# An encoder layer whose two feed-forward parts become 2x2x2 block products with seven multiplications, the residual stream with tokens on partitions

## The chip, the cores and the metric

The kernel runs on one core of a Trainium2 chip. Five engines work from their own instruction streams: PE multiplies matrices, DVE and ACT do elementwise work (only they and PE reach PSUM), POOL does elementwise work on SBUF alone, SP issues the transfers. The metric is the device time of one execution in microseconds (us).

## The reference, cut to what matters

512 tokens (two groups of 256) of 1024 channels go through one layer. The change concerns the two feed-forward parts and what touches the residual `x`; attention, the state-space branch and the memory branch stay.

```python
D_MODEL, D_FF = 1024, 2816
def rms_norm(x, g):
    y = xf * lax.rsqrt(jnp.mean(xf * xf, axis=-1, keepdims=True) + RMS_EPS)
    return y * g
def swiglu(x, w_gate, w_up, w_down):
    return (jax.nn.silu(x @ w_gate) * (x @ w_up)) @ w_down

x = x + 0.5 * swiglu(rms_norm(x, ffn1_norm), ffn1_w_gate, ffn1_w_up, ffn1_w_down)
u = rms_norm(x, mix_norm); proj = u @ w_in
...
x = x + merged @ w_out
x = x + 0.5 * swiglu(rms_norm(x, ffn2_norm), ffn2_w_gate, ffn2_w_up, ffn2_w_down)
```

## The kernel before

**Precision.** Every large product is made of three matmuls: each float32 operand is split into `hi`, its value rounded to the type fp32r, and `lo`, the rest; the product is hi·hi + hi·lo + lo·hi. A weight chunk of 128 x 1024 is loaded (`wr`, L211), cast to `wh` on ACT (L224) and the rest `wl = wr - wh` is made on DVE (L225, recorded under the helper's line L160). `ahead` (L215) does this up to two chunks ahead of PE. `wh` and `wl` have three buffers each, so the split of chunk c+2 can begin only when PE has finished chunk c-1.

**Layout.** Channels are on partitions and all 512 tokens are columns. `unit` (L372) computes 128 output channels by 512 tokens: the weights are the stationary operand, the activations stream 512 columns. `quad` (L388) is the other way round, tokens stationary and 512 weight columns streaming, one bank for each of four blocks of 128 tokens.

**Feed-forward.** Each of the two has two halves of 11 blocks of 128 hidden channels. For each block `do_g` (L406) and `do_u` (L421) take 8 k-tiles of 3 matmuls; then eight `do_d` units (L439) take 11 k-tiles of 3. The norm is not applied first: the gain alone scales x (`split_gain`, L186), matmuls begin at once, and the row factor R (`t_R`, L362: sums of squares over partitions by matmuls, a chain of small DVE operations in `rsqrt`, L192, spread back by matmuls) multiplies the results in the evacuations.

**Order.** `run` (L262) goes through a plan: a unit is written, then the evacuation of the unit before it, then one step of each side task (`step`, L233). The engines do not run in this written order: a scheduler of the framework orders each engine's instructions by when their inputs are ready, with the written order as priority. After ffn1 come the memory keys and values (`km`, `vm`), which `t_mem` (L455) prepares beside the last down products, then `dt`, which needs u (`t_u`, L478). Ahead of ffn2 stand the eight units of `do_wo` (L807). PSUM has eight banks, five for `unit` and `quad` results and three for the rest.

Of the kernel before, what the change touches and what calls it, by code (L numbers as in the profile page):

```python
# [14 lines left out]
D = 1024  # L15
NT = 512
KD = 8
DFF = 2816
HALF = 11
# [8 lines left out]

def make_plan():
    """Order in which the weights are used: (kind, key, [(matrix, k0, nk, column, width)])."""  # L30
    s = []

    def a(kind, key, mat, col, ks=((0, 8),), m=128):
        s.append((kind, key, [(mat, k0, nk, col, m) for k0, nk in ks]))

    def quad(kind, q, mat, col):
        for c in range(4):
            s.append((kind, (q, c), [(mat, 2 * c, 2, col, 512)]))

    def ffn(f):  # L40
        for hf in range(2):
            for j in range(HALF * hf, HALF * hf + HALF):
                a("g", (f, j), f + "_w_gate", j * 128)
                a("u", (f, j), f + "_w_up", j * 128)
            k0 = HALF * hf
            for m in range(8):
                a("d", (f, hf, m), f + "_w_down", m * 128, ks=((k0, 6), (k0 + 6, 5)))
# [37 lines left out]
    for m in range(8):  # L85
        a("wo", m, "w_out", m * 128)
# [5 lines left out]
CHUNKS = [c for _, _, cs in PLAN for c in cs]  # L92
OFFS = np.concatenate([[0], np.cumsum([128 * nk * m for _, _, nk, _, m in CHUNKS])])
WTOTAL = int(OFFS[-1])
# [3 lines left out]
for _name, _w in (("ffn1", 8), ("mix", 8), ("mem", 8), ("ffn2", 8), ("cw", 160), ("cb", 32), ("qn", 1), ("kn", 1),  # L98
                  ("mqn", 2), ("mkn", 2), ("sn", 16), ("dd", 16), ("dtb", 1), ("al", 1)):
    PCOLS[_name] = _n  # L100
    _n += _w
# [4 lines left out]
KEEP, EARLY = 6, 4  # L106
TEMPS = set("rw e f e2 ca cb xt yq dg jk jn pm pmT nt npT bi st qbd kT nv mq ut xgh xgl".split())


class Layer:  # L110
    def __init__(self, tc, ctx, aps):
# [5 lines left out]
        self.pg = pool("pg", 58)  # L117
        self.pt = pool("pt", 21)
        self.pw = pool("pw", 3)
# [6 lines left out]
        self.hold = False  # L126
# [4 lines left out]
        self.raw, self.split = {}, {}  # L131
        self.n_dma = self.n_split = 0
# [12 lines left out]
    def bank(self, p="m"):  # L145
        pl = self.pm if p in "mq" else self.pd
# [6 lines left out]
    def link(self, n=1):  # L153
        """Emits links of a chain of small dependent operations between larger ones."""
# [37 lines left out]
    def rsqrt(self, src, n, inv):  # L192
        """1 / sqrt(src * inv + eps), queued as a chain."""
# [11 lines left out]
    def fetch(self, upto):  # L205
        while self.n_dma <= min(upto, len(CHUNKS) - 1):
            i = self.n_dma
            _, _, nk, _, m = CHUNKS[i]
            t = self.pw.tile([128, 1024], F32, tag="raw", name=self.name("wr"))
            src = self.a["w"][int(OFFS[i]):int(OFFS[i + 1])].rearrange("(p n) -> p n", p=128)  # L210
            self.nc.sync.dma_start(out=t[:, :nk * m], in_=src)  # L211
            self.raw[i] = t
            self.n_dma += 1

    def ahead(self, ci):  # L215
        """Loads the weights up to four chunks and splits them up to two chunks ahead of chunk ci."""
        for i in range(self.n_split, min(ci + 3, len(CHUNKS))):
            self.fetch(i + 2)
            _, _, nk, _, m = CHUNKS[i]
            n = nk * m  # L220
            t = self.raw.pop(i)
# [4 lines left out]
            v = lambda z: z[:, :n].rearrange("p (k m) -> p k m", k=nk)  # L226
# [6 lines left out]
    def step(self):  # L233
        """One step of every side task in flight."""
# [27 lines left out]
    def run(self):  # L262
        self.setup()
        ci = 0
        for kind, key, chunks in PLAN:
# [3 lines left out]
            evac = getattr(self, "do_" + kind)(key, list(range(ci, ci + len(chunks))))  # L269
            ci += len(chunks)  # L270
            if not self.hold:
                self.evacuate()
# [848 lines left out]
```

## Time and profile before

| | |
|---|---|
| median of 3 runs | 1789.96 us (1789.89 to 1790.35) |
| profiled execution: span from the first to the last instruction | 1788.7 us |
| PE busy | 1775.4 us, 8240 matmuls |
| DVE busy | 1050.8 us |
| ACT busy | 743.7 us |
| POOL busy | 8.4 us |
| DMA | 196.26 MB, mean 110 GB/s |
| ffn1 (7.3 to 365 us), ffn2 (1424 to 1788.7 us) | 357.7 and 364.7 us |

The profiled execution's span is 1.3 us under the median of the timed runs; the prediction adds that to a sum made on the span. Recorded durations of matmuls overlap (390 ns each, one every 227 ns), so the cost of a matmul is read from the distance of their starts. Busy time of PE is the union of these durations.

### The profile page before, as it was taken

What the parts mean: (1) busy time and instruction counts of PE and PEld (TensorE: products, weight loads), DVE (VectorE), ACT (ScalarE), POOL (GpSimd) and SP (SyncE); (2) the same over time, 40 slices, a digit from 0 to 9 for tenths busy, and PEclk for the clock granted to TensorE, in tenths of its full rate; (3) what the DMA queues carried; (4) which work ended last, traced back from release to release, by engine and by line L of the source; (5) the groups of instructions that cost most, each with busy time, mean ns of one, the idle gap of its engine ahead of it and who ended that gap; (6) DMA issues with size and microseconds to landing.
All of it is one profiled execution on the core that took longest, in us unless ns stands there. A gap on an engine that the chain in (4) does not pass through costs nothing.

```text
span 1788.7 us, 21660 instructions
## 1 busy us (share of the span) xinstructions
PE 1775.4 (99%) x8240; PEld 1452.9 (81%) x8240; DVE 1050.8 (59%) x1904; ACT 743.7 (42%) x1376; POOL 8.4 (0%) x20
## 2 busy tenths in 40 slices
PE   8999999999999999999999999999999999999999
PEld 6888888888788888888777777777788888888887
DVE  6443444575554476867778888888743554334432
ACT  5222222443223435444656766667532432222321
POOL 0000000000000000000000000000000000000000
PEclk9999999999999999999999999999999999999999
DMA  5223322532323233333334343334343223233322
GB/s 191 96 77 101 111 102 77 177 124 78 98 81 105 73 116 100 104 89 105 124 119 127 120 136 125 135 105 155 126 161 103 94 95 95 81 115 99 95 92 85
DMA packets 74808, 196.26 MB, mean 110 GB/s; under 512 B 7632, under 2 KB 17104, under 8 KB 74704
## 3 DMA queue, kind: packets, MB, share of 16 engines
q1 hardware_dynamic: 74704, 194.87, 33.9%
q8 instruction: 65, 1.06, 0.3%
q14 instruction: 39, 0.32, 0.1%
HBM read 185.27 MB, written 9.57 MB: 109 GB/s over the span
## 4 chain that ended last, share of the span: by engine, by line
PE 99%; DVE 1%; DMA 0%; issue 0%; ACT 0%; SPq 0%; DVEq 0%
PE m L382 25%; PE m L384 25%; PE m L383 25%; PE q L400 5%; PE q L401 5%; PE q L402 5%; PE y L996 2%; PE CB L946 1%; PE ns L712 1%; PE no L735 1%; PE amo L608 1%; PE am L580 1%; PE R L359 1%; PE sum L342 1%; PE xT L935 0%; PE tr L567 0%
## 5 line engine op out<-in xcount | busy, mean ns | idle before, releaser
L224 ACT CAST wh<-wr 128x1024 fp32r<-128x1024 f32 (+2 forms) x313 | 311.1, 994 | 850.0 <-PE m L383 372.3
L160 DVE TENSOR_TENSOR wl<-wr,wh 128x1024 fp32r<-128x1024 f32 (+2 forms) x313 | 360.8, 1153 | 277.6 <-ACT wh L224 269.8
L382 PE MATMUL m<-xgh,wh 128*128 128x512 f32 x704 | 275.3, 392 | 7.3 <-ACT xgh L175 7.3
L383 PE MATMUL m<-xgl,wh 128*128 128x512 f32 x704 | 274.9, 391 | 0.5 <-DVE xgl L171 0.5
L384 PE MATMUL m<-xgh,wl 128*128 128x512 f32 x704 | 275.0, 391 | 0.0
L382 PE MATMUL m<-uh,wh 128*128 128x512 f32 (+1 forms) x584 | 234.6, 402 | 1.4 <-ACT tg L175 1.4
L383 PE MATMUL m<-ul,wh 128*128 128x512 f32 (+1 forms) x584 | 228.6, 391 | 0.0
L384 PE MATMUL m<-uh,wl 128*128 128x512 f32 (+1 forms) x584 | 228.6, 391 | 0.0
L382 PEld LDWEIGHTS m<-xgh,wh 128*128 128x128 f32 x704 | 132.6, 189 | 35.2 <-ACT xgh L175 7.9
L383 PEld LDWEIGHTS m<-xgl,wh 128*128 128x128 f32 x704 | 132.6, 188 | 29.1 <-DVE xgl L171 1.6
L384 PEld LDWEIGHTS m<-xgh,wl 128*128 128x128 f32 x704 | 132.6, 188 | 27.3
L382 PE MATMUL m<-hh,wh 128*128 128x512 f32 x352 | 137.1, 389 | 0.0
L383 PE MATMUL m<-hl,wh 128*128 128x512 f32 x352 | 137.1, 389 | 0.0
L384 PE MATMUL m<-hh,wl 128*128 128x512 f32 x352 | 137.1, 389 | 0.0
L382 PEld LDWEIGHTS m<-uh,wh 128*128 128x128 f32 (+1 forms) x584 | 109.3, 187 | 30.6 <-ACT wh L224 3.5
L384 PEld LDWEIGHTS m<-uh,wl 128*128 128x128 f32 (+1 forms) x584 | 109.3, 187 | 25.6 <-issue 1.5
L383 PEld LDWEIGHTS m<-ul,wh 128*128 128x128 f32 (+1 forms) x584 | 109.4, 187 | 22.0
L400 PE MATMUL q<-wh,uh 128*128 128x512 f32 x256 | 102.0, 398 | 0.0
L402 PE MATMUL q<-wl,uh 128*128 128x512 f32 x256 | 100.0, 391 | 0.0
L401 PE MATMUL q<-wh,ul 128*128 128x512 f32 x256 | 99.9, 390 | 0.0
L175 ACT ACTIVATE e<-rw,lots 128x256 f32<-128x256 f32 (+1 forms) x256 | 97.5, 444 | 0.0
L171 DVE SCALAR_TENSOR_TENSOR cv<-m,params,cv 128x508 f32<-128x508 f32 (+1 forms) x128 | 95.0, 742 | 1.1 <-ACT cv L175 0.2
(200 smaller groups left out, 2524.1 us busy)
## 6 DMA issues: line engine op xcount, KB each, us to landing
wr<-in_w SPq DMA_DIRECT2D x248, 512.0 KB
rw<-scr_r SPq DMA_DIRECT2D x64, 256.0 KB
wr<-in_w SPq DMA_DIRECT2D x32, 384.0 KB
wr<-in_w SPq DMA_DIRECT2D x32, 320.0 KB
nv<-scr_v SPq DMA_DIRECT2D x64, 64.0 KB
scr_o<-cv SPq DMA_DIRECT2D x12, 256.0 KB
or<-scr_o SPq DMA_DIRECT2D x12, 256.0 KB
x<-in_xT SPq DMA_DIRECT2D x8, 256.0 KB
```

The source lines that it names most:

```text
L160: self.V.tensor_tensor(out=out, in0=a, in1=b, op=op)
L171: self.V.scalar_tensor_tensor(out=out, in0=a, scalar=s, in1=b, op0=op0, op1=op1)
L175: self.S.activation(out=out, in_=x, func=f, **kw)
L224: self.S.copy(hi[:, :n], t[:, :n])
L342: self.T.matmul(ps[:, t:t + 1], acc[:, t * 128:(t + 1) * 128], self.ones[:, 0:1], start=i == 0, stop=i == len(accs) - 1)
L382: self.T.matmul(ps[:m], wh[:, kk, :], xh, start=i == 0, stop=False)
L383: self.T.matmul(ps[:m], wh[:, kk, :], xl, start=False, stop=False)
L384: self.T.matmul(ps[:m], wl[:, kk, :], xh, start=False, stop=i == n - 1)
L400: self.T.matmul(self.qb[t], xh, wh[:, kk, :], start=k == 0, stop=False)
L401: self.T.matmul(self.qb[t], xl, wh[:, kk, :], start=False, stop=False)
L402: self.T.matmul(self.qb[t], xh, wl[:, kk, :], start=False, stop=k == KD - 1)
L996: T.matmul(yb[64 * hp:64 * hp + 64, b * 256:(b + 1) * 256], xt[i][:, (2 * b + st) * 128 + 64 * hp:(2 * b + st) * 128 + 64 * hp + 64], w[hp ...
```

## The change

A block of rows of W is split by input halves, a block of columns by output halves (for gate and up: the up block is output half 0, the gate block output half 1), and the tokens by halves of 256. The 2x2x2 product then takes seven half-size products in place of eight (the Winograd form: 4 sums of activation blocks, 4 of weight blocks, 7 of results). D_FF is walked in six column blocks, five of 512 and one of 256; each has a `gu` unit and then a `dn` unit of seven products in the order 1, 2, 6, 5, 7, 3, 4. Weight sums are made on POOL, out of ten ring buffers; activation sums on DVE and POOL (`t_second`); the sums of results partly by accumulating into a bank that holds an earlier product, partly in evacuations. Weight and hidden blocks are 128 x 1024 per item as before, but an item now serves 256 tokens: 12 matmuls of 512 columns (gate and up in the 256 block: 24 of 256 columns).

The residual lives as four tiles of 128 tokens in two halves of 512 channels. Norms are applied ahead of the products: sums of squares along the free axis on ACT, the same `rsqrt` chain, one multiply on DVE, then PE transposes and splits. `do_wo` becomes `quad`, in three parts (all tokens for channels 0 to 511, then tokens 0 to 255 and 256 to 511 for the rest). Pool `pg` shrinks from 58 to 51 buffers.

```diff
+CBLOCKS = ((0, 512), (512, 512), (1024, 256), (1280, 512), (1792, 512), (2304, 512))
+RING = 10
+PRODUCTS = (1, 2, 6, 5, 7, 3, 4)
+BANKS = {1: "A", 2: "D", 6: "A", 5: "C", 7: "A", 3: "C", 4: "A"}
+def seven(kind, key, block, nh):
...
+            loads, subs = {1: (["B11"], []), 2: (["B21"], []),
+                           6: (["B12", "B22"], [("T1", "B12", "B11"), ("T2", "B22", "T1")]), 5: ([], []),
+                           7: ([], [("B12", "B22", "B12")]), 3: ([], []), 4: ([], [("T2", "B21", "T2")])}[p]
+            src = {1: "B11", 2: "B21", 6: "T2", 5: "T1", 7: "B12", 3: "B22", 4: "T2"}[p]
...
     def ffn(f):
-        for hf in range(2):
-            for j in range(HALF * hf, HALF * hf + HALF):
-                a("g", (f, j), f + "_w_gate", j * 128)
-                a("u", (f, j), f + "_w_up", j * 128)
...
+        for ci, (c0, w) in enumerate(CBLOCKS):
+            n, j0 = w // 256, c0 // 128
+            s.extend(seven("gu", (f, ci), lambda i, j, h: (f + ("_w_up", "_w_gate")[j], 4 * i + 2 * h, 4 // n, c0, w), n))
+            s.extend(seven("dn", (f, ci), lambda i, j, h: (f + "_w_down", j0 + n * i, n, 512 * j, 512), 1))
...
+    def make(self, upto):
...
+                    self.G.tensor_tensor(out=t[:, :it.nk * it.m], in0=a, in1=b, op=ALU.subtract)
...
     def setup(self):
...
+        self.load_x(0)
+        dma(out=self.consts[:, :128], in_=self.a["consts"][:, :128])
+        gain = self.gains(0)
+        self.load_x(1)
+        self.make(1)
+        self.load_x(2)
+        self.load_x(3)
+        self.make(3)
...
+        self.start_ffn("ffn1", gain)
+        self.require(("X", "ffn1", 0))
...
+    def t_norm(self, ts, gain, dst):
...
+                self.act(j, self.x[t][hf], AF.Square, accum_out=ss[:, hf * n + i:hf * n + i + 1])
+        self.tt(sm, ss[:, :n], ss[:, n:2 * n], ALU.add)
+        r = self.rsqrt(sm, n, 1.0 / D)
...
+                self.stt(y, self.x[t][hf], r[:, i:i + 1], gain[hf], ALU.mult, ALU.mult)
...
+    def t_first(self, tr, n, s, f):
+        for i in range(2):
+            ps = tr(i)
+            s[i + 1].append(self.split_ps(ps[:, :n], n, "s"))
+            t = self.g(p="af")
+            self.S.copy(t[:, :n], ps[:, :n])
...
+    def t_second(self, tr, n, s, f, k):
...
+        self.S.copy(a21[:, :n], ps[:, :n])
+        ps = tr(1)
+        self.tt(s1[:, :n], ps[:, :n], a21[:, :n], ALU.add)
+        self.tt(s2[:, :n], s1[:, :n], a11[:, :n], ALU.subtract)
+        s[6].append(self.split_n(s2, n, "s"))
+        s[5].append(self.split_n(s1, n, "s"))
+        self.G.tensor_tensor(out=s3[:, :n], in0=a11[:, :n], in1=a21[:, :n], op=ALU.subtract)
+        self.G.tensor_tensor(out=s4[:, :n], in0=a12[:, :n], in1=s2[:, :n], op=ALU.subtract)
+        yield
+        s[7].append(self.split_n(s3, n, "s"))
+        s[3].append(self.split_n(s4, n, "s"))
+        s[4].append(self.split_ps(ps[:, :n], n, "s"))
...
+    def product(self, key, cis, left, w):
...
+        for t in range(2):
+            ps = self.acc[b][t]
+            for kk in range(nk):
+                xh, xl = (z(kk, t) for z in left)
...
+                go(xh, wh[:, kk, :], start=first, stop=False)
+                go(xh, wl[:, kk, :], start=False, stop=False)
+                go(xl, wh[:, kk, :], start=False, stop=last)
...
+    def do_gu(self, key, cis):
...
+                if p in (1, 6, 5):
+                    self.S.copy(o[p, t][:, :w], v)
...
+                if p == 4:
+                    self.tt(y[:, :w], v, y[:, :w], ALU.mult)
...
+                self.tt(y[:, :w], v, o.pop(({2: 1, 7: 5, 3: 6}[p], t))[:, :w], ALU.add)
...
+                    self.act(y[:, :w], y[:, :w], AF.Silu)
...
+                    self.tt(y[:, :w], y[:, :w], o.pop(("sg1", t))[:, :w], ALU.mult)
...
+    def t_h(self, r, o, w, hs, hf):
...
+                    self.T.transpose(ps[i][:, kt * 256 + t * 128:kt * 256 + t * 128 + 128], y[:, c:c + 128], self.ident)
...
+    def pre_dn(self, key):
+        f, ci, p, h, nh = key
+        if p == 1:
...
+            self.require(("h", f, ci, 0))
+            if f == "ffn1" and ci == len(CBLOCKS) - 1:
+                self.xs = None
+                self.later("mem", self.t_mem())
+        if p == 6:
+            self.require(("h", f, ci, 1))
+    def do_dn(self, key, cis):
...
+                if p in (1, 6, 5):
+                    self.act(o[p, t], ps[t], AF.Copy, scale=0.5)
...
+                self.stt(x, ps[t], 0.5, x, ALU.mult, ALU.add)
+                if q:
+                    self.G.tensor_tensor(out=x, in0=x, in1=y, op=ALU.add)
...
+    def do_wo(self, key, cis):
+        q, c = key
+        ts = ((0, 1, 2, 3), (0, 1), (2, 3))[q]
+        qb = self.quad(key, cis, self.merged, ts)
...
+            if q == 1:
+                self.start_ffn("ffn2", self.gains(2))
...
```

## Rows read from the trace of the kernel before

**Rows 1.** The page: busy time by engine; the chain that ended last.

```profile
PE 1775.4 (99%) x8240; PEld 1452.9 (81%) x8240; DVE 1050.8 (59%) x1904; ACT 743.7 (42%) x1376; POOL 8.4 (0%) x20
...
PE 99%; DVE 1%; DMA 0%; issue 0%; ACT 0%; SPq 0%; DVEq 0%
```

**Rows 2.** Busy time by stretch: ffn1, ffn2; stretch: length, busy us (xinstructions), clock, DMA.

```profile
7.30:365.00 357.70, 357.20 (x1571) 294.66 (x1572) 171.81 (x227) 115.82 (x155) 0.00 (x0) 1.00 0.35 116
...
1424.00:1788.70 364.70, 360.85 (x1600) 298.83 (x1598) 152.54 (x197) 95.51 (x121) 0.00 (x0) 1.00 0.30 94
```

**Rows 3.** Timeline of one up unit in ffn1: start us, duration us, engine, instruction.

```profile
99.71 0.39 PE L382 MATMUL m<-xgh,wh 128*128 128x512 f32 x1
99.73 1.06 ACT L224 CAST wh<-wr 128x1024 fp32r<-128x1024 f32 x1 [3.86 <-issue]
99.92 0.69 DVE L160 TENSOR_TENSOR h<-m,sl 128x512 f32<-128x512 f32 x1 [2.71 <-PE m L384]
...
100.69 0.62 ACT L182 CAST hh<-h 128x512 fp32r<-128x512 f32 x1
100.82 1.23 DVE L160 TENSOR_TENSOR wl<-wr,wh 128x1024 fp32r<-128x1024 f32 x1 [0.21 <-ACT wh L224]
...
101.96 0.68 DVE L160 TENSOR_TENSOR hl<-h,hh 128x512 fp32r<-128x512 f32 x1
...
105.15 0.39 PE L382 MATMUL m<-xgh,wh 128*128 128x512 f32 x1
```

**Rows 4.** Groups of matmuls by form: count, busy us, mean ns, idle before.

```profile
L382 PE MATMUL m<-xgh,wh 128*128 128x512 f32 x704 | 275.3, 392 | 7.3 <-ACT xgh L175 7.3
...
L382 PE MATMUL m<-hh,wh 128*128 128x512 f32 x352 | 137.1, 389 | 0.0
```

**Rows 5.** The page: the group of weight loads of one matmul line.

```profile
L382 PEld LDWEIGHTS m<-xgh,wh 128*128 128x128 f32 x704 | 132.6, 189 | 35.2 <-ACT xgh L175 7.9
```

**Rows 6.** Timeline: eight transposes and the first load behind them.

```profile
519.75 0.94 PEld L567 LDWEIGHTS tr<-consts,qr 128*128 128x128 f32 x8
...
520.66 0.19 PEld L400 LDWEIGHTS q<-wh,uh 128*128 128x128 f32 x1
```

**Rows 7.** Timeline: the two matmul groups of one R.

```profile
374.70 0.97 PEld L342 LDWEIGHTS sum<-consts,sq 128*128 128x128 f32 x8 [0.30 <-DVE sq L160]
...
378.89 0.97 PEld L359 LDWEIGHTS R<-dg,consts 128*128 128x128 f32 x8 [0.26 <-issue]
```

**Rows 8.** Timeline of DVE: two operations behind each other.

```profile
127.11 0.69 DVE L160 TENSOR_TENSOR gp<-m,R 128x512 f32<-128x512 f32 x1 [3.19 <-PE m L384]
127.72 0.81 DVE L160 TENSOR_TENSOR wl<-wr,wh 128x640 fp32r<-128x640 f32 x1
```

**Rows 9.** Groups by form on ACT, and all that POOL does of any length.

```profile
L175 ACT ACTIVATE sl<-gp 128x512 f32<-128x512 f32 x44 | 27.5, 625 | 7.6 <-DVE gp L160 7.6
...
L937 ACT COPY xt<-xT 128x512 f32<-128x512 f32 x16 | 8.5, 576 | 0.2
...
L681 POOL MEMSET qbd<- 128x512 f32 x16 | 8.2, 526 | 762.1 <-PE tr L567 567.2 <-PE ns L712 68.1 <-PE no L735 47.2
```

**Rows 10.** Timeline of the start on PE and ACT.

```profile
7.28 0.79 PE L382 MATMUL m<-xgh,wh 128*128 128x512 f32 x1 [7.28 <-ACT xgh L175]
...
9.17 0.63 PE L384 MATMUL m<-xgh,wl 128*128 128x512 f32 x1
9.60 0.63 PE L382 MATMUL m<-xgh,wh 128*128 128x512 f32 x1
...
7.86 1.38 ACT L175 ACTIVATE xgh<-x,params 128x512 fp32r<-128x512 f32 x2 [0.64 <-DMA x<-in_xT]
```

**Rows 11.** Timeline of DVE: first and tenth of the eleven links of `rsqrt`.

```profile
24.06 0.15 DVE L196 TENSOR_SCALAR v<-sum 128x4 f32<-128x4 f32 x1
...
25.83 0.16 DVE L201 SCALAR_TENSOR_TENSOR t<-t,v 128x4 f32<-128x4 f32 x1
```

**Rows 12.** Waits: who waited for whom, us in total, times, longest.

```profile
ACT wh L224 <- PE m L383: 372.3, 134, 6.2
```

More of the change, by code (lines that the diff above doesn't have):

```diff
@@ L84, in make_plan @@
         branch("ssd", j)
-    for m in range(8):
-        a("wo", m, "w_out", m * 128)
+    quad("wo", 0, "w_out", 0)
+    quad("wo", 1, "w_out", 512)
+    quad("wo", 2, "w_out", 512)
     ffn("ffn2")
@@ L222, in ahead, with drop @@
+    def drop(self, *names):
+        for n in names:
+            self.left[n] -= 1
+            if not self.left[n]:
+                del self.live[n]
+    def ahead(self, ci):
+        for i in range(self.n_split, min(ci + 3, len(ITEMS))):
+            it = ITEMS[i]
+            self.make(i)
+            self.make(i + self.depth)
+            n = it.nk * it.m
+            t = self.live[it.src]
             hi = self.pw.tile([128, 1024], F32R, tag="hi", name=self.name("wh"))
@@ L268, in run @@
                 pre(key)
[L269 to L272, printed above, removed]
+            evac = getattr(self, "do_" + kind)(key, items)
+            self.evacuate()
             if evac:
@@ new lines, in start_ffn, with t_x, tr @@
+    def start_ffn(self, f, gain):
+        self.xs, self.xf = {p: [] for p in PRODUCTS}, ([], [])
+        self.active.append((("X", f, 0), self.t_x(0, gain), (), 0))
+        self.queue.append((("X", f, 1), self.t_x(1, gain), (("X", f, 0),) + (("x2",) if f == "ffn2" else ()), -1))
+    def t_x(self, r, gain):
+        xn = {}
+        yield from self.t_norm((2 * r, 2 * r + 1), gain, xn)
+        if r == 0:
+            yield
+        for k in range(2):
+            def tr(i):
+                ps = self.bank("xT")
+                for kt in range(2):
+                    ch = 4 * i + 2 * k + kt
+                    for t in range(2):
+                        o = kt * 256 + t * 128
+                        self.T.transpose(ps[:, o:o + 128], xn[2 * r + t][ch // 4][:, ch % 4 * 128:(ch % 4 + 1) * 128], self.ident)
+                return ps
+            yield from (self.t_second(tr, 512, self.xs, self.xf, k) if r else self.t_first(tr, 512, self.xs, self.xf))
@@ new lines, in t_h @@
+    def t_h(self, r, o, w, hs, hf):
+        n = w // 256
+        yield
+        ps = [self.bank("hT") for _ in range(2)]
+        for t in range(2):
+            y = o.pop(("h", r, t))
+            for i in range(2):
+                for kt in range(n):
+                    c = (n * i + kt) * 128
+                    self.T.transpose(ps[i][:, kt * 256 + t * 128:kt * 256 + t * 128 + 128], y[:, c:c + 128], self.ident)
+            if t == 0:
+                yield
+        tr = lambda i: ps[i]
+        yield from (self.t_second(tr, w, hs, hf, 0) if r else self.t_first(tr, w, hs, hf))
```

393 lines of the change are left out of this document (236 added, 157 removed).

## The prediction

> **What bounds the kernel now.** I read the page's busy times first: PE is busy for 1775 of 1788.7 us, and the chain that ended last runs over PE for 99% [rows 1]. The clock was full in both feed-forward stretches, which take 357.7 and 364.7 us, and in them DVE was busy for under half of the time and POOL not at all [rows 2]. The reader is to see two things there: a microsecond of PE taken from these stretches is a microsecond of the whole, as long as nothing else becomes late, and what the change adds goes to engines that have room in the old proportions only.
>
> The duration of a matmul is not its cost. In the timeline of one unit, 24 matmuls lie between 99.71 and 105.15 us [rows 3]: 0.2267 us from start to start, though each is shown with 0.39. The two layers hold (704 + 352) x 3 = 3168 of them [rows 4], so 718.2 us, which fits the stretches. The same rows show who works beside: one cast (0.96 us from its start to the next operation's), one split `wl` on DVE (1.14) for every 5.44 us of PE. They show too that an engine doesn't keep the written order: `h` belongs to an evacuation written behind that split, and runs first. So I don't cost waits by the written order, but by what depends on what.
>
> **PE's work.** Per layer the five 512 blocks take 7 x 24 matmuls of 512 columns for gate and up and 7 x 12 for down, 252; the 256 block takes 168 of 256 columns and 42 of 512. Two layers: 2604 x 0.2267 = 590.3 us, and 336 of 256 columns. For these the trace has no row. Half the price would be 0.113; eight transposes, each with a load of 128 columns, follow each other in (520.66 - 519.75) / 8 = 0.114 us [rows 6], so loads go that fast; if a load could not be covered, its duration of 0.189 [rows 5] is the other end. I take 0.12, near the transposes, where loads are as dense: 40.3 us (38 to 64).
>
> Transposes are added: 64 for the normed x, 176 for the hidden blocks, 32 for u; 272 x 0.114 = 31.0. Three R go, 2 x 0.97 each [rows 7]: 5.8. Nothing else on PE moves: `do_wo` has 192 matmuls either way. PE thus has 718.2 + 5.8 - 590.3 - 40.3 - 31.0 = 62.4 us less to do, not the 90 of an eighth. Per 512 block it is 252 x 0.2267 + 16 x 0.114 = 58.9 us (before, 288 matmuls, 65.3), per 256 block 30.6 (before 32.6).
>
> **What the other engines get for it.** An item of weights serves 256 tokens in place of 512, so the splitting of weights per PE time doubles. In a 512 block DVE has 21 splits x 1.14 = 23.9, and 27 operations of 512 elements (ten evacuating gate and up, two and seven in `t_first` and `t_second`, eight evacuating down) at 0.61, the distance of two such [rows 8], = 16.5: 40.4 of 58.9 us. ACT has 21 x 0.96 + 26 x 0.6 [rows 3, 9] = 35.8. Both fit. In the 256 block DVE has 7 x 1.14 + 15 x 0.61 + 19 x 0.35 (256 elements, by the slope between the two prices) = 23.8 of 30.6.
>
> POOL gets, per 512 block, 12 subtractions of 1024 elements and 8 operations of 512. The trace has no such row. Its only work is a memset of 512 in 0.526 us [rows 9], which reads nothing. From below, two operands cost no more than that; from above, two reads and a write pass one after the other, 1.58. I take two passes, 1.05 (2.1 for 1024), since a memset is one pass and two operands have to be read: 33.6 us per block, 57% of PE's time (16.8 to 50.4). By this alone POOL bounds nothing, and its subtractions are written five items, some 13 us, ahead.
>
> The Trainium skill (GPSIMD Engine Reference, section 3.1) gives 4497 ns for a two-input float32 operation of 2048 elements; an estimate by it is 2.25 us for 1024 and 35.5 per block, and no row here shows one.
>
> **Whether POOL and DVE can read side by side** decides the sign. DVE reads two SBUF tensors in `wl` as fast per element as one SBUF and one PSUM tensor in `gp` [rows 3, 8], so it has two paths; whether POOL reads by one of its own no row shows, as POOL never read. The ends: full overlap leaves PE's 58.9 as the bound. Full exclusion of POOL and those DVE operations that read two SBUF tensors (21 splits and 7 of 512, 28.2 us) gives 28.2 + 33.6 = 61.8 us of turns in a 512 block, already over PE's. The 12.2 us of DVE operations that read PSUM may lie beside POOL; if none do, the block takes 74.0. I take two thirds of them beside it, as POOL runs ahead and mostly has work queued: 65.9. For the 256 block: 14.8 + 20.0 = 34.8, at most 43.8, taken 37.8. I count it as excluded, because in the old trace the cover that it would need has never been used, and because an item's split has only two items, 5.4 us, of slack, of which cast and split take 2.1 and one subtraction in front of it another 2.1.
>
> The Trainium skill (SBUF — State Buffer, section "Who interferes with whom") says that a DVE instruction with two SBUF inputs and a GpSimd instruction that reads SBUF exclude each other for the whole instruction. By that rule the block could not go under the sum of the turns; without it, PE's time would stand. No run here shows either.
>
> **Starts.** Ffn1 begins at 7.28 us now, because matmuls take the unnormed x [rows 10]. Now two x tiles, the identity and the gains (1.6 MB) come first; the third x tile, with 1.4 MB in front of it and in it, was there at 7.86 [rows 10], so 8.9. Then two squares at 0.8, eleven links at 0.2 [rows 11], three multiplies at 0.66, four transposes at twice their price, 0.9, since the first matmuls stand 0.43 us apart [rows 10], and a cast of 0.6: first matmul at 16.4, 9 us later (6 to 16). At ffn2 the first half's norm is covered by the last four `do_wo` items, 10.9 us; the second half's chain (squares 2.4, links 2.2, multiplies 2.6, transposes and sums 3) is as long as products 1 and 2: 2 us (0 to 8). `t_mem`, some 21 us of DVE and ACT work together, now lies beside 20 us of down products where it had 57: 3 us (0 to 10). Together 14. The tail, one multiply-add and one transfer behind the last matmul, stays. SP's queue moves the same bytes but for 2 MB of `w_out` that is loaded twice and the gains; with DMA at 0.35 that is nothing, and if it weren't, the casts would show waits for `wr`.
>
> **Sum.** 10 x 65.9 + 2 x 37.8 = 734.6, the x transposes 7.3, u's 3.6 less its R of 1.9, the starts 14: 757.6, in place of 718.2 + 3.9. That is 35.5 more: span 1824.2, and with the 1.3 us between span and median 1825 us. From the lower to the upper end of the turns it would be 1778 to 1919.
>
> **Rivals.**
> First, POOL and DVE don't disturb each other. Then a block costs PE's time and a wait at the change from gate and up to down: multiplies, transposes, copy, two sums and a cast make 4.5 us against 5.4 of products 1 and 2, so little is left, 1.5. 10 x 60.4 + 2 x 32.1 + 23 - 722.1 = -31: 1759 us, faster. For it: DVE, ACT and POOL each stay below 70%. It decides for the other side where turns take less than 58.9 us per block, for example at a subtraction of 1.9 us.
> Second, still without exclusion, waits on banks. In a down unit product 6 adds to the bank of product 1, with one item (2.72 us) of cover for a cast and two copies (2.2), and product 4 to that of product 7, with the same cover for a split and two multiply-adds (2.4). A cast ACT waits for PE to finish an old chunk, 372 us in all [rows 12], so such orders are tight. One cast and split more in front (2.1) at both places cost 3.5: 5 per block, 1801 us. Against it: the engines take what is ready first.
> Third, POOL at its upper price, 1.58: turns of 28.2 + 49.8 and POOL the bound, some 82 and 46 us per block, near 2003.
>
> **How the numbers follow.** Forecast 0.44, the first rival 0.33, the second 0.13, the third 0.05, 0.05 for what lies between. No row settles the exclusion, so neither side gets more than half. The first rival is faster in nearly all of its chance (0.31), the forecast's lower end adds 0.05, the second 0.01: 0.37 faster by over 0.2%, about what a measurement of this kernel can tell from no change, 0.06 within, 0.57 slower. The range leaves out a tenth on each side: 1744, where the first rival's starts are at their low end, to 1870, between the middle and the upper end of the turns. The forecast's own range is 1778 to 1870.
>
> **What would show it.** Steps are right if matmuls of 256 columns start 0.12 us apart, the first matmul comes near 16 us, and splits `wl` beside POOL's subtractions last up to twice their 1.23 us, with PE waiting for `wl`. The exclusion is wrong if splits keep 1.23 us next to a running subtraction; the forecast is wrong too if a subtraction takes far from 2.1 us, or if PE's waits stand in front of products 6 and 4 for banks rather than splits.

## The result and the profile after

The changed kernel takes 1945.85 us (median of 4 runs, 1945.21 to 1953.72) against 1790.1 us of the kernel before: a ratio of 1.0879, 95% interval 1.0861 to 1.0898. It is slower by 155.7 us. The prediction had said slower, 1825 us, with a range up to 1870; the sign and the mechanism came out as forecast, the size did not. Each experiment below but gu7c is one run; the changed kernel's four runs differ by up to 8.5 us, so what is smaller than that is read from the stretches of the traces.

The page's busy times and the chain, where [rows 1] had PE for 99%:

```profile
PE 1790.4 (92%) x8236; PEld 1442.0 (74%) x8236; DVE 1463.0 (75%) x2149; ACT 967.4 (50%) x1738; POOL 568.0 (29%) x260
...
PE 72%; DVE 16%; issue 5%; POOL 4%; ACT 2%; DMA 1%; SPq 0%; ACTq 0%; DVEq 0%; POOLq 0%
```

28% of the chain is no longer PE's, 16% is DVE's. PE's busy time even rose by 15 us with 62 us less to do; a matmul at the lower clock is shown with 0.63 us in place of 0.39.

Busy time by stretch (length, then busy us of PE, PEld, DVE, ACT, POOL, clock, DMA share, GB/s): the start, ffn1, all that lies between, ffn2; then one regular 512 block, its gate and up stretch and its down stretch:

```profile
0.00:18.60 18.60, 2.95 (x12) 2.13 (x13) 6.96 (x19) 7.00 (x13) 0.20 (x4) 1.00 0.80 301
18.60:454.00 435.40, 367.13 (x1588) 293.27 (x1587) 367.53 (x323) 219.96 (x317) 275.56 (x118) 0.91 0.28 94
454.00:1518.45 1064.45, 1056.29 (x5066) 856.79 (x5065) 735.64 (x1498) 531.71 (x1111) 26.13 (x24) 1.00 0.36 114
1518.45:1942.00 423.55, 364.05 (x1577) 289.81 (x1575) 352.92 (x313) 208.69 (x299) 266.16 (x116) 0.92 0.24 76
```

```profile
305.66:349.31 43.65, 41.31 (x177) 33.35 (x176) 33.48 (x28) 21.12 (x27) 27.62 (x10) 0.96 0.33 109
349.31:377.63 28.32, 23.05 (x93) 18.07 (x92) 26.14 (x22) 14.59 (x21) 21.35 (x11) 0.88 0.17 56
```

Next to [rows 2] the two layers, 435.4 and 423.6 us, are most of the difference: 137 of the 156 us. This block takes 72.0 us for the 58.9 us of PE work that the prediction counted, and in its down stretch DVE is busy for 26.1 and POOL for 21.4 of 28.3 us.

The groups that the change made dear (xcount | busy us, mean ns of one | idle before):

```profile
L208 DVE TENSOR_TENSOR wl<-wr,wh 128x1024 fp32r<-128x1024 f32 x388 | 609.9, 1579 | 299.3 <-ACT wh L297 293.9 <-PE xT L1172 2.5 <-PE tr L794 1.5
L208 DVE TENSOR_TENSOR sl<-sf,sh 128x512 fp32r<-128x512 f32 x56 | 83.2, 1530 | 1.4 <-ACT sh L431 1.4
L219 DVE SCALAR_TENSOR_TENSOR x<-ac,x 128x512 f32<-128x512 f32 x96 | 62.8, 678 | 2.7 <-PE ac L542 2.7
...
L275 POOL TENSOR_TENSOR wr<-wr,wr 128x1024 f32<-128x1024 f32 x128 | 361.5, 2831 | 888.7 <-DVE wl L208 814.9 <-DMA wr<-in_w 63.2 <-DVE t L249 6.2
```

`wl` lasted 1.23 us in [rows 3] and lasts 1.58 on average now. `sl<-sf,sh`, which reads two SBUF tensors, has more than doubled from the 0.68 us that an operation of its size takes; `x<-ac,x`, which reads PSUM and one SBUF tensor, still takes 0.68.

The timelines of DVE and POOL in the same down stretch (start us, duration us) show why:

```profile
353.85 1.79 DVE L208 TENSOR_TENSOR wl<-wr,wh 128x1024 fp32r<-128x1024 f32 x1 [1.77 <-ACT wh L297]
...
356.16 0.68 DVE L219 SCALAR_TENSOR_TENSOR x<-ac,x 128x512 f32<-128x512 f32 x1
356.76 1.85 DVE L208 TENSOR_TENSOR sf<-sf,af 128x512 f32<-128x512 f32 x1
...
360.75 4.52 DVE L208 TENSOR_TENSOR sl<-sf,sh 128x512 fp32r<-128x512 f32 x2
```

```profile
352.16 2.40 POOL L275 TENSOR_TENSOR wr<-wr,wr 128x1024 f32<-128x1024 f32 x1 [11.50 <-DVE wl L208]
355.72 2.35 POOL L275 TENSOR_TENSOR wr<-wr,wr 128x1024 f32<-128x1024 f32 x1 [1.16 <-DVE wl L208]
358.02 1.72 POOL L457 TENSOR_TENSOR sf<-af,af 128x512 f32<-128x512 f32 x1
359.70 3.34 POOL L275 TENSOR_TENSOR wr<-wr,wr 128x1024 f32<-128x1024 f32 x1
```

POOL's first subtraction ends at 354.56; the split that was issued at 353.85 ends 1.08 us later, so it waited for POOL's end and then took about its usual time (1.14 us from start to start in [rows 3]). The sum `sf` that was issued at 356.76 ends 0.54 us after POOL's second subtraction, again about its own time. `x<-ac,x`, with its PSUM operand, runs through beside POOL. It goes the other way round as well: POOL's subtraction of 359.70 lasts 3.34 us, where the eight that have no DVE operation beside them last 2.38 to 2.40.

PE waits behind that, in front of product 6 (start us, duration, [idle before]):

```profile
359.81 0.79 PE L542 MATMUL ac<-wh,sh 128*128 128x512 f32 x1 [3.93 <-ACT s L223]
363.65 0.79 PE L542 MATMUL ac<-wh,sl 128*128 128x512 f32 x1 [1.33 <-DVE sl L208]
...
392.16 0.50 PE L542 MATMUL ac<-wh,sh 128*128 128x512 f32 x1 [0.76 <-ACT wh L297]
394.49 0.79 PE L542 MATMUL ac<-wl,sh 128*128 128x512 f32 x1 [1.83 <-DVE wl L208]
```

The first two are product 6 of the down layer (the copies `s` of product 1's bank stand on ACT behind casts that wait for these sums), the last two product 6 of the next gate and up, whose weights T1 and T2 POOL subtracts while the down stretch keeps it busy. After such a stop the next six or so matmuls stand 0.43 us apart in place of 0.23, the lower level of the clock (1.2 GHz), and the granted clock of the down stretch is 0.88 where it was 1.00.

### The profile page after: what moved, and what is told of

Its sections match the earlier page's. It is cut to its first block, busy times and chain, and to the rows that moved or that the text cites. A ratio compares the mean times of both kernels' runs of the same rounds, so it can differ in the third digit from the quotient of the medians.

```text
span 1944.4 us, 22742 instructions
## 1 busy us (share of the span) xinstructions
PE 1790.4 (92%) x8236; PEld 1442.0 (74%) x8236; DVE 1463.0 (75%) x2149; ACT 967.4 (50%) x1738; POOL 568.0 (29%) x260
## 4 chain that ended last, share of the span: by engine, by line
PE 72%; DVE 16%; issue 5%; POOL 4%; ACT 2%; DMA 1%; SPq 0%; ACTq 0%; DVEq 0%; POOLq 0%
PE ac L542 19%; PE m L521 10%; PE m L523 10%; PE m L522 10%; DVE wl L208 6%; PE q L566 5%; PE q L568 5%; PE q L567 5%; DVE sl L208 4%; POOL wr L275 3%; PE y L1233 2%; DVE sf L208 1%; ACT wh L297 1%; DVE x L219 1%; POOL x L670 1%
## 5 line engine op out<-in xcount | busy, mean ns | idle before, releaser
L208 DVE TENSOR_TENSOR wl<-wr,wh 128x1024 fp32r<-128x1024 f32 (+1 forms) x403 | 626.6, 1562 | 304.8 <-ACT wh L297 299.3
L297 ACT CAST wh<-wr 128x1024 fp32r<-128x1024 f32 (+1 forms) x403 | 414.9, 1034 | 645.2 <-PE ac L542 200.7
L275 POOL TENSOR_TENSOR wr<-wr,wr 128x1024 f32<-128x1024 f32 (+1 forms) x136 | 375.7, 2770 | 909.8 <-DVE wl L208 835.7
L542 PE MATMUL ac<-wh,sh 128*128 128x512 f32 (+1 forms) x980 | 395.1, 404 | 55.5 <-ACT s L223 38.3
L542 PE MATMUL ac<-wl,sh 128*128 128x512 f32 (+1 forms) x980 | 390.9, 399 | 24.9 <-DVE wl L208 24.9
L542 PE MATMUL ac<-wh,sl 128*128 128x512 f32 (+1 forms) x980 | 390.4, 401 | 21.8 <-DVE sl L208 21.8
L542 PEld LDWEIGHTS ac<-wh,sh 128*128 128x128 f32 x980 | 196.1, 200 | 102.0 <-ACT s L223 44.7
L542 PEld LDWEIGHTS ac<-wh,sl 128*128 128x128 f32 x980 | 196.5, 201 | 69.0 <-DVE sl L208 32.0
L542 PEld LDWEIGHTS ac<-wl,sh 128*128 128x128 f32 x980 | 196.6, 201 | 67.4 <-DVE wl L208 31.4
L208 DVE TENSOR_TENSOR sl<-sf,sh 128x512 fp32r<-128x512 f32 (+1 forms) x64 | 96.1, 1540 | 1.4 <-ACT sh L431 1.4
```

The costliest lines, as they stand in the source:

```text
L208: self.V.tensor_tensor(out=out, in0=a, in1=b, op=op)
L275: self.G.tensor_tensor(out=t[:, :it.nk * it.m], in0=a, in1=b, op=ALU.subtract)
L297: self.S.copy(hi[:, :n], t[:, :n])
L542: go = lambda l, r, **f: self.T.matmul(ps[:, :w], l, r, skip_group_check=True, **f)
```

## The theories and the experiments

Theory A: a POOL operation that reads SBUF and a DVE operation that reads two SBUF tensors exclude each other, and the turns are longer than PE's work. Rivals: B, POOL's sums are late by their own length, disturbed or not; C, waits on banks and ACT's order. Two versions of A part later: A1, the sum of turns over a block decides, as the prediction reckoned; A2, it decides in each stretch for itself. Two smaller questions stand beside them: what the lower clock costs, and why the first blocks are so long.

The table was worked out from the records of these runs. "Pair" is the time in which DVE, or POOL with a sum, is busy, counted once; the means are over six of the 512 blocks, without the first and the last of each layer. PE's work is 58.9 us per block (61.7 for gu7): 39.0 and 19.9 (22.7 for gu7) in the two stretches.

```
kernel      time     block   gate and up: length, pair   down: length, pair
changed     1945.9   74.1          45.1   42.4              28.9   28.0
half        1842.7   66.9          41.5   33.0              25.3   23.0
noread      1810.9   63.2          40.6   26.1              22.6   18.2
direct      1912.5   70.0          40.3   38.2              29.7   28.7
balanced    1905.6   69.1          39.3   34.9              29.8   28.6
pool4       1879.6   67.8          41.8   37.8              26.0   24.1
all_dve     1845.9   64.9          40.8   37.7              24.1   22.3
warm        1937.3   73.0          43.4   41.5              29.5   28.3
gu7         1815.1   62.7          39.3   27.1              23.4   16.4
```

**noread: POOL as busy, but not reading.**

```
# n stands for it.nk * it.m
-self.G.tensor_tensor(out=t[:, :n], in0=a, in1=b, op=ALU.subtract)
+self.G.tensor_tensor(out=t[:, :8], in0=a[:, :8], in1=b[:, :8], op=ALU.subtract)
+self.fill(t, 8, n, 2340 * n // 1024)   # memsets of so many columns in all
...
```

> Every subtraction and addition on POOL is replaced by one over 8 columns, which keeps what waits for what, and by memsets that last about as long (2.4 us in place of a subtraction of 1024 elements, 1.2 in place of one of 512), so POOL is as busy and its results as late, but it reads almost nothing; the sums of blocks are left out. Theory A (POOL and the DVE operations with two SBUF inputs exclude each other while POOL reads): splits wl beside POOL are back at 1.23 us, the regular 512 blocks go from 72-76 us to 60-62, the time to 1790-1820. Theory B (POOL's own time per sum, bunched in the down stretch, is the bound): the waits in front of products 6 stay, 1900-1950. Theory C (banks and ACT's order): stays over 1900 with DVE undisturbed.

Measured: 1810.9 us, in theory A's range (its blocks, 63.2 us, are a little over the 60 to 62). Timelines of DVE and POOL at the start of a down stretch:

```profile
302.56 1.23 DVE L208 TENSOR_TENSOR wl<-wr,wh 128x1024 fp32r<-128x1024 f32 x1 [0.41 <-ACT wh L305]
305.57 1.22 DVE L208 TENSOR_TENSOR wl<-wr,wh 128x1024 fp32r<-128x1024 f32 x1 [1.78 <-ACT wh L305]
```

```profile
300.43 2.37 POOL L285 MEMSET wr<- 128x1016 f32 x3 [14.40 <-DVE sg L208]
303.86 0.20 POOL L275 TENSOR_TENSOR wr<-wr,wr 128x8 f32<-128x8 f32 x1 [1.06 <-DVE wl L208]
304.00 2.37 POOL L285 MEMSET wr<- 128x1016 f32 x3
...
307.92 0.73 POOL L275 TENSOR_TENSOR wr<-wr,wr 128x8 f32<-128x8 f32 x1
```

Splits keep 1.22 us beside a memset that runs all through them; the mean of all `wl` is 1223 ns again. Even POOL's sum over 8 columns, 0.20 us by itself, takes 0.73 while DVE's `sf<-sf,af` of 307.91 holds it off. So 135 of the 156 us hang on POOL's reading, and theory A stands; B falls as the main cause. The sign does not hang on it: without the reading the kernel is still 20.4 us slower than the one before that ran beside it (1790.5). What C says is there too, but small: PE still stops for 2.2 us in front of down product 6, for the copies of product 1's bank, and a block takes 63.2 us, 4.3 over PE's work. 2.7 of this lie in the down stretches; the rest lies in the two blocks behind the 256 block, where the casts of weights wait for POOL's fills, so there B is seen as well.

**half: reading for half of the time.**

```
+w = it.nk * it.m // 2
+self.G.tensor_tensor(out=t[:, :w], in0=a[:, :w], in1=b[:, :w], op=ALU.subtract)
+self.fill(t, w, 2 * w, 1170 * w // 512)
...
```

> Every operation on POOL sums only one half of its columns and fills the other half with a constant for as long as the sum would take, so POOL is as busy and as late as in the changed kernel but reads for half of the time; the sums of the other halves are left out. Theory A1 (the sum of turns over a block decides, as in the prediction): 28.2 + 19.3 = 47.5 us of turns per 512 block, below PE's 58.9, so nearly all of the 135 us between the changed kernel and the one without reading is gone, 1810-1830. Theory A2 (each read costs where it falls, as the down stretch of 20 us has no room for it): about half of the 135 us stays, 1865-1890.

Measured: 1842.7 us, between the ranges of A1 and A2, which both miss. Of the 135 us three quarters are gone with half of the reading, so it isn't a price per read; but 32 us stay although the pair's 56 us per block are below PE's 58.9. The table says where: the down stretch still takes 25.3 us for 20 of PE, with the pair busy for 23.0 of them, while gate and up are back near 39 in most blocks. So A1 is right that turns add up and that room for them counts, A2 that the room in one stretch does not serve another.

**all_dve, direct, balanced, pool4: where the sums are made.** All on DVE; the down copies and additions replaced by a multiply-add from the bank; the same and half of the weight subtractions on DVE; all on DVE but four subtractions per block.

```
# all_dve, at L275, L457, L458, L670
-self.G.tensor_tensor(...)
+self.V.tensor_tensor(...)
# direct, for products 1, 6 and 5 too, and no copy and no addition of y
+self.stt(x, ps[t], 0.5, x, ALU.mult, ALU.add)
# balanced = direct, and L457, L458 on DVE, and
+e = self.V if it.subs[0][0].endswith("T1") else self.G
# pool4 = all_dve, but POOL keeps B12 and T2 of gate and up's products 7 and 4
```

> All twelve subtractions and eight additions of a block move from POOL to DVE, at 1.23 and 0.68 us each, undisturbed: DVE then has 40.4 + 12 x 1.23 + 8 x 0.68 = 60.6 us per 512 block against 58.9 of PE. Theory A: more work for the engine that PE waits for, yet a shorter block, 62-66 us in place of 73, and 1830-1870. If DVE's amount of work and not the exclusion sets the block: DVE would have 20 us more of it, and the time would be over 1946.

> Down products 1, 6 and 5 are added to x by DVE straight from their PSUM bank, the same multiply-add that the other four get; six copies on ACT and six POOL additions per block go, DVE gets six operations of 0.68 us that read one SBUF tensor. POOL keeps twelve subtractions of 2.4-2.8 us and two of 512. Theory A: per block 10 us less of POOL reading in the down stretch and no ACT copy behind it; the waits in front of down products 6 and the next gate and up products 6 shrink from about 9 us per block to 3-5, block 65-68, time 1860-1890. If POOL's weight subtractions alone make the waits: over 1920.

> As the kernel in which down products are added straight from the bank, and in addition the subtractions T1 and T2 for product 6 (six per block) and the two of 512 in the second half go to DVE; POOL keeps the six for products 7 and 4. DVE 40.4 + 6 x 0.68 + 6 x 1.23 + 2 x 0.68 = 53.2 us per 512 block, turns of two-input DVE operations and POOL 28.2 + 8.7 + 6 x 2.38 = 51.2. Theory A: both below PE's 58.9, blocks of 60-63 us, time 1795-1830. If a full DVE queue holds evacuations back whatever POOL does: 1850 and over.

> All sums on DVE (1845.9) but for four of the twelve weight subtractions per block, those of gate and up for products 7 and 4, which stay on POOL. DVE 60.6 - 4 x 1.23 = 55.7, POOL 9.5 us per block, turns of POOL and two-input DVE operations about 53. Theory A1 (sum over the block): now everything is below PE's 58.9, blocks of 61-63 us, 1810-1830. Theory A2: a read of 2.38 us on POOL in the down stretch holds back DVE for longer than the 1.23 us that it saves there; no better than all sums on DVE, 1845-1880.

Measured: 1845.9, 1912.5, 1905.6 and 1879.6 us. All sums on DVE came out as expected: 20 us more work per block for DVE, and 100 us less time. Pool4 lies at the slow end of A2's range, and A1's (1810 to 1830) is out. Direct missed on the slow side, between its two ranges, and balanced lies where its rival had it: a full DVE queue, 1850 and over. Balanced has 69.5 us of DVE and POOL in all by the prices, less than the changed kernel's 81.2, and its gate and up stretches are perfect; but the multiply-adds and T1, T2 went into the down stretch. One block of each, gate and up, then down:

```profile
291.40:330.60 39.20, 39.20 (x178) 32.27 (x177) 32.67 (x32) 21.39 (x27) 8.06 (x3) 1.00 0.37 121
330.60:362.90 32.30, 25.06 (x93) 19.33 (x92) 27.48 (x32) 11.37 (x15) 7.16 (x3) 0.84 0.14 49
```

```profile
270.60:311.00 40.40, 39.87 (x177) 31.93 (x176) 37.12 (x41) 21.13 (x26) 0.00 (x0) 1.00 0.33 117
311.00:336.10 25.10, 22.28 (x93) 17.52 (x93) 22.43 (x29) 14.30 (x21) 0.00 (x0) 0.93 0.18 64
```

The first pair of lines is balanced, the second all_dve. In balanced's down stretch DVE is busy for 27.5 of 32.3 us with three subtractions on POOL, in all_dve's for 22.4 of 25.1 with none: DVE's own work weighs there, and not only the turns. And pool4 shows what one subtraction on POOL does (DVE, POOL, PE):

```profile
338.80 3.40 DVE L276 TENSOR_TENSOR wr<-wr,wr 128x1024 f32<-128x1024 f32 x1
342.12 1.21 DVE L208 TENSOR_TENSOR wl<-wr,wh 128x1024 fp32r<-128x1024 f32 x1
```

```profile
337.96 3.15 POOL L276 TENSOR_TENSOR wr<-wr,wr 128x1024 f32<-128x1024 f32 x1 [41.84 <-DVE wr L276]
```

```profile
343.39 0.50 PE L543 MATMUL ac<-wl,sh 128*128 128x512 f32 x1 [2.83 <-DVE wl L208]
```

DVE's own subtraction waits 2.2 us for POOL, the split queued behind it too, and PE gets `wl` 2.8 us late. A subtraction on POOL saves DVE 1.23 us, and this one took 2.2 from it. So A2 in this form: in each stretch the pair's time is a bound of its own. In every row of the table where the pair has over 21 us of the down stretch, that stretch is 0.9 to 2.3 us longer than the pair. This is read from nine kernels; none of them moves the pair's time alone.

**warm: what the lower clock costs.**

```
+if p == 6 and CBLOCKS[ci][1] == 512:
+    self.dummies(18, self.hs[1][0][0])     # 12 before gate and up's first product 6
```

> The changed kernel, all of its work on POOL as it is, with PE given matmuls of no use in each 512 block: 18 (4.1 us) in front of down product 6, 12 (2.7 us) in front of the first product 6 of gate and up, where it stands idle for about 4.3 and 3.5 us. Their results are read by nobody. If the half clock after each stop (about 5.5 us per block lost in matmuls that stand 0.43 us apart) is a cost of its own, PE does 6.8 us more per block and the time falls all the same, by 3-5 us per block, to 1895-1915. If the clock costs nothing because DVE and POOL are behind anyway: 1940-1965.

Measured: 1937.3 us, between the two ranges; 1.1 us less per block in place of 3 to 5, in all about as much as the changed kernel's runs differ. PE in the stretch that begins at 345.3:

```profile
351.73 4.24 PE L556 MATMUL dm<-sh 128*128 128x512 f32 x18
355.86 0.50 PE L542 MATMUL ac<-wh,sh 128*128 128x512 f32 x1
356.19 0.40 PE L542 MATMUL ac<-wl,sh 128*128 128x512 f32 x1
359.70 0.50 PE L542 MATMUL ac<-wh,sl 128*128 128x512 f32 x1 [3.11 <-DVE sl L208]
360.03 0.39 PE L542 MATMUL ac<-wh,sh 128*128 128x512 f32 x1
360.26 0.40 PE L542 MATMUL ac<-wl,sh 128*128 128x512 f32 x1
```

The clock did what was meant: matmuls behind the stop are back at 0.23 us apart after one step of 0.33, and the mean clock rose from 0.960 to 0.980. But `sl` comes 14.4 us after the stretch's start here and 14.3 in the changed kernel (363.65 less 349.31). In the changed kernel the matmuls that stand too far apart lose 5.1 us per block by their starts, in warm 2.5. So of 2.6 us won from the clock about one was kept, and the rest was lost in the next wait: my theory that 3 to 5 us per block come back falls. What the other half of the clock's loss is worth no run shows.

**gu7: seven products in gate and up only, ordinary ones in down, all sums on DVE.**

```
-s.extend(seven("dn", (f, ci), ...))
+for j in range(2):
+    for c in range(n):
+        s.append(("dn", (f, ci, j, c, n), [plain(f + "_w_down", j0 + 2 * c, 2, 512 * j, 512)]))
...
# the sums and their splits of the hidden blocks go; left is, for each of two transposed blocks,
+hs[r].append(self.split_ps(ps[i][:, :w], w, "s"))
```

> All sums on DVE, and only gate and up as seven products; the down layer as eight ordinary block products (96 matmuls of 512 columns per block in place of 84). PE per 512 block 39.0 + 21.8 + 1.8 for transposes = 61 in place of 58.9; DVE 18 x 1.23 + 8 x 1.23 + 10 x 0.68 + 4 x 0.68 + 8 x 0.68 = 47 in place of 60.6. If DVE's load in the down stretch is what all sums on DVE leaves as a loss: blocks of 62-63 us and 1805-1825, below all sums on DVE in spite of more PE work. If the seventh product saves in the down layer what it should: 15-25 us over all sums on DVE, 1860-1870.

Measured: 1815.1 us, as expected, 31 below all_dve with 2.7 us more of PE work per block.

```profile
261.20:300.40 39.20, 39.20 (x178) 32.26 (x177) 26.53 (x28) 21.14 (x26) 0.00 (x0) 1.00 0.41 134
300.40:323.70 23.30, 22.84 (x105) 18.80 (x104) 18.01 (x22) 5.29 (x6) 0.00 (x0) 1.00 0.13 46
```

PE is busy for 62.0 of 62.5 us and the clock is full. With this the regular blocks are settled; what is left over the kernel before lies at the start and in the first blocks, 83.4 and 77.8 us.

**early, tuned7: the start, and all at once.** In both, x's second tile is loaded first and the second half's norm begins beside the first's; tuned7 also has all sums on DVE, the multiply-adds from the bank and the memory branch prepared a stretch earlier.

```
-self.queue.append((("X", f, 1), self.t_x(1, gain), (("X", f, 0),) + ..., -1))
+self.active.append((("X", f, 1), self.t_x(1, gain), (), 0))
...
```

> The changed kernel with two differences at the start: the second x tile is loaded ahead of the identity and the gains, and in ffn1 the norm of tokens 256 to 511 begins beside that of tokens 0 to 255 in place of behind it. If the late norms are what makes ffn1's first block 20 us longer than the others, the first matmul comes at 14-15 us (18.6 before) and the first block takes 78-84 us (95.9 before): 1926-1935. If POOL's turns make that block long: at most 4 us less, 1940-1946.

> Seven products in both layers, all sums on DVE, down products added to x straight from their bank, the early start, and the memory branch's preparation begun during the last gate and up stretch in place of the last down stretch. Against all sums on DVE (1845.9): start -4, first block of ffn1 -12, copies of ACT out of the way of down product 6 -1 per block, memory preparation -5: 1812-1828. If DVE's 60.6 us per block is the bound everywhere, only the first two count: 1828-1835.

Measured: 1940.8 and 1857.0 us. Early lies where its rival had it (1940 to 1946), tuned7 over both of its ranges. The first matmul came at 21.7 us in place of 18.6. DVE in early:

```profile
7.18 0.16 DVE L208 TENSOR_TENSOR sm<-ss 128x2 f32<-128x2 f32 x1 [7.18 <-ACT jk L223]
11.57 2.53 DVE L208 TENSOR_TENSOR wl<-wr,wh 128x1024 fp32r<-128x1024 f32 x2 [4.23 <-ACT wh L297]
15.34 0.16 DVE L208 TENSOR_TENSOR sm<-ss 128x2 f32<-128x2 f32 x1 [1.24 <-ACT jk L223]
15.41 0.16 DVE L244 TENSOR_SCALAR v<-sm 128x2 f32<-128x2 f32 x1
```

The first half's sum `sm` is there at 7.18, but its chain of small operations was written behind the second half's `sm`, which needs the third and fourth x tiles: 8 us lost on an engine with little to do. The edit was at fault, so early does not speak for its rival either, and these runs leave the first block open. tuned7 agrees on the down stretch: moving the copies to DVE made it 25.8 to 27.9 us in six regular blocks where all_dve has 22.1 to 25.1.

**gu7b, gu7c: the first block again.** gu7b is gu7 with the norm of the second half one step behind the first's, its chain in one piece, x's second tile first, and ordinary gate and up products in the first block, so that the second half is needed 10.9 us later. gu7c takes up single waits on top of that.

```
+if now:
+    self.link(99)                       # the eleven small operations at once
...
+s.append(("fo", (f, r, j, i, hh, 4 // n), [plain(f + ("_w_up", "_w_gate")[j], 4 * i + 2 * hh, 4 // n, c0, w)]))
```

> Seven products in gate and up only, all sums on DVE (1815.1), and each ffn's first 512 block with ordinary gate and up products (192 matmuls in place of 168, 4.5 us more of PE), so that tokens 256 to 511 are needed 21.8 us after the first matmul in place of 10.9; their norm starts earlier, its chain of eleven small operations is not spread between other work, and the second x tile is loaded ahead of the gains. If the late second half alone makes the first blocks 20 and 15 us too long: first matmul at 14-15 (18.9), first blocks 68-70 us (83.4 and 77.8), 1780-1792. If POOL-free DVE is still what they wait for: 1800-1810.

> The last kernel (1793.7) with PE's remaining waits taken up: the raw halves of tokens 256 to 511 are split ahead of their sums (2.7 us of waits in ffn2's first block), the first channels of both token blocks are normed first (1.3 us at the start), the hidden blocks' second transposes are written one step earlier (0.7 us of wait per block, ten blocks), the memory branch's preparation begins a stretch earlier (2.2 us before the last down products). If PE is the bound, each wait comes back in full: 1781-1787, below the kernel before (1790.4). If something else follows right behind: 1790-1794, no difference from the kernel before.

Measured: gu7b 1793.7 us, 2 over its range; first matmul at 14.3 us, first blocks 73.2 and 73.7 us with 5.4 us more of PE work in them (24 matmuls at 0.2267; the 4.5 expected is too low). First block of the changed kernel, of gu7 and of gu7b:

```profile
18.60:114.50 95.90, 72.10 (x291) 56.65 (x290) 86.46 (x81) 48.85 (x75) 57.71 (x26) 0.86 0.25 86
```

```profile
18.90:102.20 83.30, 70.19 (x302) 56.07 (x301) 67.71 (x92) 39.54 (x60) 0.00 (x0) 0.92 0.29 99
```

```profile
14.30:87.50 73.20, 72.08 (x324) 58.33 (x325) 59.45 (x83) 40.75 (x60) 0.00 (x0) 1.00 0.53 189
```

So 15.5 of the 20.7 us by which gu7's first block exceeds a regular one (10.1 gained, 5.4 of added work on top) were the second half's late norm, its chain and its due time together; the norm ahead of the first product brings that with it. Which of the three weighs most no run parts. gu7c missed: 1799.1 us in the median of five runs, 1.0049 times the kernel before (1.0036 to 1.0063). Putting the raw halves first left all sums to follow on DVE in one run, and PE waited for a split that stood behind them:

```profile
37.16 0.79 PE L634 MATMUL ac<-wl,sh 128*128 128x512 f32 x1 [5.51 <-DVE wl L218]
```

No version ran below the kernel before; gu7b, with one run, is 3.3 us over it, less than the 4.2 us by which gu7c's five runs differ.

## Why the prediction was right in kind and wrong in size

**Right.** PE's work was counted well: matmuls of 256 columns stand 0.12 us apart (194.79, 194.91, 195.03 in the 256 block), and noread's gate and up stretches take 39.2 us in most blocks, for 39.0 counted. The exclusion is there; splits beside POOL last up to 3.43 us, PE waits for `wl`, `sl` and for copies queued behind both. The Trainium skill (SBUF — State Buffer, section "Who interferes with whom") names just this pair and calls such contention an exclusive lock; the split of 353.85, which ends 1.08 us after POOL's operation, agrees. In noread a POOL memset, which only writes, holds off no split. No row had settled the exclusion: it was chosen at 0.44 against 0.46 for the two rivals without it, so that it holds is partly luck. And it "decides the sign" only by the prediction's own sum: noread has no such turns and is still slower than the kernel before. The third rival, POOL at 1.58 us per 512 elements, is out. The second is there with 4.3 us per block, next to its 5: its stop in front of product 6 is seen, the one in front of product 4 is not. Without the exclusion it would have been the nearest, 1801 against noread's 1810.9, with the first blocks' excess, below, on top.

**The first step that failed: the block at 65.9 us.** Eight blocks, all but the first of each layer, take 74.1 us on average, 8.2 more: 65 of the 120 us by which the forecast missed. By its own terms: the operations that read two SBUF tensors are 29.3 us (DVE is busy for 42.4 us per block in noread, 13.1 of them with PSUM), predicted 28.2. POOL's work is 12 x 2.38 + 8 x 1.28 = 38.8, predicted 33.6 (2.38 is what one takes alone, 1.28 what the subtractions of 512 columns take alone in half): "two passes" was too cheap. By the Trainium skill's 4497 ns for 2048 elements (GPSIMD Engine Reference, section 3.1) an estimate is 2.25 us for 1024 and, for 16 of them, 36.0 per block (the prediction's 35.5 is half a microsecond short); the 2.38 and 38.8 measured are a little over it. Of the PSUM operations 7.4 us lie beside POOL in the records, 56% where two thirds were taken, so 5.7 don't. 29.3 + 38.8 + 5.7 = 73.8. So the sum of turns was the right formula here, where the pair has more to do than PE in both stretches, with a POOL price 13 to 22% too low; the down stretch adds that it can't be spread, as half and pool4 showed. That 73.8 meets 74.1 so closely is partly luck: an operation that was held off ends sooner after its release than it lasts by itself (0.54 us for `sf`, 0.68 alone), and by the table the pair is busy for 70.4 us (42.4 and 28.0), not 73.8; in the other 3.7 neither works.

**The second: the starts at 14 us.** The first blocks of the layers take 95.9 and 87.4 us; the prediction gave them the price of any block and 2 us, so 49 us too little: 16 of that is the block price again, 33 their own excess. It had reckoned the second half's norm in ffn2 as covered by products 1 and 2, and has no term for it in ffn1. In the changed kernel PE waits for it twice in ffn1:

```profile
39.95 0.45 PE L482 MATMUL xT<-consts,xn 128*128 128x128 f32 x1 [8.19 <-DVE xn L219]
...
51.90 0.79 PE L542 MATMUL ac<-wh,sh 128*128 128x512 f32 x1 [5.79 <-ACT sh L431]
```

The chain's eleven links were priced at 0.2 us each, 2.2 in all, and the four multiplies behind them at 2.6. In the changed kernel the links take 7.4 us (29.63 to 37.04), and the multiplies 6.8. The two links shown and the multiplies have two SBUF inputs as well, and POOL's subtractions hold them off like a split, though a link has two columns only. DVE there, and the same multiplies in noread:

```profile
32.22 2.33 DVE L248 TENSOR_TENSOR t<-y 128x2 f32<-128x2 f32 x1
34.59 2.26 DVE L249 SCALAR_TENSOR_TENSOR t<-t,v 128x2 f32<-128x2 f32 x1
...
37.08 6.80 DVE L219 SCALAR_TENSOR_TENSOR xn<-x,y,gb 128x512 f32<-128x512 f32 x4
```

```profile
31.42 2.74 DVE L219 SCALAR_TENSOR_TENSOR xn<-x,y,gb 128x512 f32<-128x512 f32 x4
```

But the exclusion is not the whole cause: in noread and gu7, where it is all but gone or gone, the first blocks are still 8 to 21 us longer than a regular one. In gu7's ffn1 the links, each written behind another DVE operation, take 10 us (29.5 to 39.8) with subtractions and splits of 1.2 us between them; in noread's ffn1 they take 3.4, and there PE waits longest, 5.9 us, for a cast of weights. How the 33 us divide is open. The first rival, 1759, failed by the same step: it lacks the exclusion as noread does, and noread is 52 us over it, 22 of them by the 4.3 against 1.5 us of waits in eight blocks, some 30 by the first blocks.

**The rest.** The 256 blocks take 41.1 and 40.9 us, predicted 37.8 (6 together, the same POOL price); the first matmul came at 18.6, predicted 16.4; between ffn1 and ffn2, and for `t_mem`, the sums nearly met. 65 + 49 + 6 + 2 is the 120 to within 3. Two slips in the prediction's sums change nothing: the terms of the first matmul's 16.4 add up to 16.2, and POOL's upper price per block is 50.4 in one place and 49.8 in another.

**The range.** It took the upper end of the turns as 74.0 and then stopped at 1870, "between the middle and the upper end". The upper end of POOL's price was held by a rival of 0.05 only, at 1.58; what lay between 1.05 and 1.58 had no place in the range, and 1.28 is there. Even the full upper end of the turns, 1919, is 27 us short of the result: its 74.0 is the measured block by another sum, and the first blocks' excess comes on top.

## What to carry to other kernels

Work that is moved to POOL is not moved off DVE's path when both read SBUF: add POOL's time to that of DVE's two-SBUF operations and compare the sum with the bound, for each stretch and not for the whole. Small operations on a chain that others wait for count too: two links of 0.16 us took 2.3 each in this trace. Here the same sums cost less on the loaded DVE (1.23 us each) than on the idle POOL (2.38 and a turn). And a saving of an eighth of the multiplications is worth what is left after the operands' sums, splits and transposes have been paid: with seven products in gate and up alone, ordinary ones in the first blocks, and nothing on POOL, it came to within 3.3 us of the kernel before, in one run, and not below it.

## What the runs showed of the hardware

POOL's two-input operation of 1024 float32 elements takes 2.38 us undisturbed, a memset of 1016 columns 0.95. A POOL memset runs beside DVE's splits without a trace in either (1.22 us of 1.23), but three one-input operations of DVE (`v<-sm`, `y<-v`), 0.17 us by themselves, lasted 0.60 to 1.02 in noread and ended with a running memset. On POOL a sum over 8 columns, 0.20 us, lasts up to 1.28 us. A DVE operation with one PSUM operand is not touched by POOL's reads (0.677 us beside, 0.68 alone). A DVE operation of two columns with two SBUF inputs, 0.16 us by itself, lasted 2.33 beside a POOL subtraction. What I had not expected: of the 2.6 us per block that matmuls put into two stops won back from the lower clock, only about 1 was kept, as `sl`, for which PE waits next, came no earlier (14.4 us into the stretch, 14.3 without them).
